# A transformer-like block on one Trainium2 core: first norm on tokens-on-partitions tiles turned by TensorE, and stores issued by the producing engine

## Chip, cores and metric

The kernel runs on 1 core of one Trainium2 chip. The metric is the device time of one execution in microseconds (us), the median of the runs shown.

## What is computed

One layer on x (1024 tokens x 1024 channels, f32), cut to what bears on the change:

```
mod = silu(c) @ w_ada + b_ada            # shift1, scale1, gate1, shift2, scale2, gate2
h   = rms_norm(x, norm1_g) * (1 + scale1) + shift1
z   = h @ w_in                           # q latent | kv latent | rope key | conv GLU input | gate logits
u   = glu_a * sigmoid(glu_b); u = causal_depthwise_conv(u) ...; y_b = silu(layer_norm(u)) @ w_pw_out
y_a = attention(...) @ w_o_mla
x   = x + gate1 * ((sigmoid(g_a) * y_a + sigmoid(g_b) * y_b) @ w_out)
x   = x + gate2 * (relu(h2 @ w_ff1) ** 2 @ w_ff2)     # h2: second norm and modulation
```

## The kernel before

Every f32 product is made of three products of rounded parts: an operand is split into `hi` (ScalarE, `copy`, L108) and `lo` = operand - `hi` (`split`, L114), and `mm` (L117) is called for hi*hi, lo*hi and hi*lo. So one result bank of 128x512 takes 3 matmuls for each 128 of depth.

**The first stage** (L289 to L390, 0 to 85 us). x is read transposed (`x_t`, channels on partitions) as eight tiles `x0..x7` of 128x1024, in two halves `c` of 512 tokens. `norm(c)` squares the eight tiles (ScalarE, L319, L322), adds the squares (VectorE, L323), sums over partitions with 8 small matmuls against ones, takes a reciprocal root on VectorE and ScalarE (`rsqrt`, L218) and spreads it to all partitions with four turns on TensorE (`spread`, L227). For each depth block k of 128 channels, `modulation(k)` reads two rows of blocks of `w_ada` (`ada_load`, 512 KB each, six buffers) and forms `sc` and `sh` on VectorE (`ada`, L282); `scaled` multiplies x by `sc` and the spread norm (L347); `h_tile(k, c)` adds `sh`, makes `hhi` (ScalarE, L353) and `hlo` (VectorE, L354) and issues the 12 matmuls for the first four output tiles, z0. For 8 k and 2 c that makes 192 matmuls into 8 banks of 512: `z` (four) and two pairs `k`.

**The next stages** (85 to 450 us): further tiles of `w_in` (`z_tile`), of which four more feed the GLU (`glu`) and the convolution (`conv`, VectorE, GpSimd, ScalarE), and the gate tiles. `gate` (L404) applies the sigmoid on ScalarE and stores it with `nc.sync.dma_start` (L409). Weight tiles are prefetched by `weights`/`fetch` (L126 to L140) with two buffers each for raw, hi and lo.

**The first MLP product** (820 to 1050 us). By a Strassen-like scheme, a step m of 16 reads two raw weight tiles (`prepare_w`, L976, `raw`, L889), forms their sums and splits on VectorE and ScalarE, and multiplies five products (seven from m = 12), each of 12 matmuls into one of six `z` banks; VectorE adds the results up (`sum_of`, L1013). `right_operands` (L1034) forms four differences on GpSimd. `keep` (L1010) stores each finished block with `nc.sync.dma_start`; `p1_d` (L1029) stores a partial product.

Each engine runs its instructions in one fixed order, written down at build time by a list scheduler. SyncE's queue does too: a DMA there waits for its data and for a free buffer, and what stands behind it waits too.

Of the kernel before, what the change touches and what calls it, by code (L numbers as in the profile page):

```python
# [17 lines left out]
S = 1024  # L18
D = 1024
# [56 lines left out]
def block_kernel(ctx: ExitStack, tc: tile.TileContext, a: dict, out: bass.AP):  # L76
# [46 lines left out]
    def plan(src, width=D, hi_eng=None, lo_eng=None):  # L123
        loads.append((src, width, hi_eng or nc.scalar, lo_eng or nc.gpsimd))
# [16 lines left out]


    for t in range(2 * KC - 4):
        plan(a["w_in"][t], lo_eng=nc.vector if t < 2 else None)
    first = [sum(FILL[:n]) for n in range(len(FILL) + 1)]

    def plan_gates(n):
# [92 lines left out]
    def halves(ts):  # L240
        return [[t[:, cs(0)], t[:, cs(1)]] for t in ts]
# [33 lines left out]
    def ada_load(j):  # L275
        w = ada_pool.tile([P, D], F32, name="wada", bufs=6)
        nc.sync.dma_start(w, a["w_ada"][blk(j)])
        return w
# [5 lines left out]
        )  # L284

    phase = ExitStack()
    phase.enter_context(psum(z=4, k=2))


    z0 = [[None, None] for _ in range(4)]  # L290
    z0_pairs = []
    with tc.tile_pool(name="xp", bufs=1, **right) as xp:
        xs = [xp.tile([P, S], F32, name=f"x{k}") for k in range(KD)]
        rs = xp.tile([P, S], F32, name="rs")
        w0 = []
        w0r = []
        aw = []

        def load_x(c):
            for k in range(KD):  # L300
                nc.sync.dma_start(xs[k][:, cs(c)], a["x_t"][blk(k)][:, cs(c)])

        def load_w(k):
            aw.append((ada_load(KD + k), ada_load(k)))
            raw = xp.tile([P, C], F32, name="w0raw", bufs=2)
            nc.sync.dma_start(raw, a["w_in0"][k])
            w0r.append(raw)
# [6 lines left out]
        def norm(c):  # L314
            acc = xp.tile([P, C], F32, name="xacc", bufs=2)
            for k in range(KD):
                x_k = xs[k][:, cs(c)]
                if k == 0:
                    nc.scalar.activation(acc, x_k, AF.Square)  # L319
                else:  # L320
                    sq = xp.tile([P, C], F32, name="sq", bufs=3)
                    nc.scalar.activation(sq, x_k, AF.Square)  # L322
                    nc.vector.tensor_tensor(acc, acc, sq, ALU.add)  # L323
            shi = xp.tile([P, C], F32R, name="shi")
            slo = xp.tile([P, C], F32R, name="slo")
            split(shi, slo, acc, nc.scalar, nc.vector)
            st, rb = halves([pair("k")])[0]
            r1 = rsqrt(xp, stat_cols(shi, slo, NB // 2, st=st), D, [P, NB // 2], f"r1{c}")
            spread(r1, [rb])
            copy(nc.scalar, rs[:, cs(c)], rb)  # L330
            return rb

        mod1 = []

        def modulation(k, rb=None):
# [3 lines left out]
            nc.vector.tensor_scalar(sc, sc, 1.0, v("g1", k), ALU.add, ALU.mult)  # L339
            mod1.append((sc, sh))  # L340
            if rb is not None:
                scaled(k, 0, rb)
            ada(sh, k, aw[k][1])

        def scaled(k, c, rb):
            x_k = xs[k][:, cs(c)]
            nc.vector.scalar_tensor_tensor(x_k, x_k, mod1[k][0], rb, ALU.mult, ALU.mult)  # L347

        def h_tile(k, c):
            sh = mod1[k][1]  # L350
            x_k = xs[k][:, cs(c)]
            hi, lo = h_hi[k][:, cs(c)], h_lo[k][:, cs(c)]
            nc.scalar.activation(hi, x_k, AF.Identity, bias=sh)  # L353
            nc.vector.scalar_tensor_tensor(lo, x_k, sh, hi.bitcast(F32), ALU.add, ALU.subtract)  # L354
            whi, wlo = w0[k]
            for m in range(4):
                if k == 0 and c == 0:
                    z0[m][c] = bank("z")
                elif k == 0:
                    if m % 2 == 0:  # L360
                        z0_pairs.append(pair("k"))
                    z0[m][c] = z0_pairs[m // 2][:, cs(m % 2)]
                o = z0[m][c]
                mm(o, whi[:, blk(m)], hi, k == 0, False)
                mm(o, whi[:, blk(m)], lo, False, False)
                mm(o, wlo[:, blk(m)], hi, False, k == KD - 1)

        load_x(0)
# [3 lines left out]
        load_x(1)  # L372
        for k in range(KD):
            load_w(k)
        rb = norm(0)
        first_norm = last_rsqrt[0]
        norm(1)
        second_norm = last_rsqrt[0]
        split_w(0)
        with tc.issue_after(first_norm.ins):  # L380
            modulation(0, rb)
        for k in range(KD):
            h_tile(k, 0)
            if k + 1 < KD:
                split_w(k + 1)
                with tc.issue_after(second_norm.ins):
                    modulation(k + 1)
                scaled(k + 1, 0, rs[:, cs(0)])
            scaled(k, 1, rs[:, cs(1)])
            h_tile(k, 1)  # L390
        sel_f = xp.tile([P, C], F32, name="sel_f", tag="sq", bufs=3)[:, 0:13 * NH + P]
# [12 lines left out]
    def gate(d, new):  # L404
        o = z_tile()
        for c in range(2):
            s_t = new("sg")
            nc.scalar.activation(s_t, o[c], AF.Sigmoid)  # L408
            nc.sync.dma_start(s_d[d][:, cs(c)], s_t)  # L409

    def gates(n, new):
        for d in range(first[n], first[n + 1]):
# [5 lines left out]
    with tc.tile_pool(name="cv", bufs=1, **right) as cv:  # L418
# [17 lines left out]
        def conv(i, u):

# [31 lines left out]
        conv(2, us[2])
# [835 lines left out]
```

## Time and profile before

| | |
|---|---|
| median of 3 runs | 1402.04 us (1401.58 to 1405.19) |
| the profiled execution | 1403.63 us, its span 1401.5 us |
| TensorE busy | 1335.7 us (95%) |
| VectorE, ScalarE, GpSimd busy | 995.6, 680.4, 402.2 us |
| mean granted TensorE clock | 0.988 |
| DMA | 234.72 MB, 167 GB/s over the span |

The span runs from the first to the last instruction; the profiled execution's own time is 2.1 us longer, and 1.6 us over the median. An engine that is busy 95% of the span bounds the kernel almost everywhere, so what counts is where it is idle or runs at a lower clock, and which other engine ends that.

### The profile page before, as it was taken

The page shows a single profiled execution, that of the slowest core. Times are in us where ns is not written, and L with a number is a line of the kernel's source. Part 1 is how long each engine was busy: PE and PEld are TensorE (multiplying, and loading weights), DVE is VectorE, ACT ScalarE, POOL GpSimd, SP SyncE. Part 2 cuts the span into 40 slices and gives each one's busy share as a digit, 9 for nine tenths or more (in the row PEclk, how much of TensorE's full clock was granted, in tenths as well). Part 3 has the DMA queues.
Part 4 walks back from the last instruction along what each step waited for, and adds up shares of the span by engine and source line. Part 5 has one row for each costly group of instructions (what it writes and reads, how often), then busy time and mean ns, then how long its engine had stood idle before and what let it go on. Part 6 is the DMA issues. An engine that isn't in the chain of part 4 may idle for free. (4 is left out here: it accounts for less than half of the span.)

```text
span 1401.5 us, 17857 instructions
## 1 busy us (share of the span) xinstructions
PE 1335.7 (95%) x6160; PEld 1088.4 (78%) x6160; DVE 995.6 (71%) x1488; ACT 680.4 (49%) x1107; POOL 402.2 (29%) x280
## 2 busy tenths in 40 slices
PE   3899999999998999999999999989999999999998
PEld 2687888887676888878788878767778887887787
DVE  7969997955346788767546788766675459848854
ACT  6345422246556777753345763343455444444342
POOL 0049932244554655425100003334333100000000
PEclk9999999999999999999999999999999999999999
DMA  9611227731475323127546555566656678633442
GB/s 358 218 45 53 84 93 277 260 121 60 137 253 188 121 91 121 47 77 259 190 135 205 188 186 208 197 195 210 211 176 234 236 227 279 215 98 90 140 139 76
DMA packets 106186, 234.72 MB, mean 167 GB/s; under 512 B 12016, under 2 KB 12272, under 8 KB 106096
## 3 DMA queue, kind: packets, MB, share of 16 engines
q1 hardware_dynamic: 106096, 233.58, 49.3%
q8 instruction: 48, 0.79, 0.2%
q14 instruction: 42, 0.34, 0.1%
HBM read 169.57 MB, written 63.96 MB: 167 GB/s over the span
## 5 line engine op out<-in xcount | busy, mean ns | idle before, releaser
L117 PE MATMUL z<-hhi,whi 128*128 128x512 f32 x384 | 152.7, 399 | 0.4 <-ACT sg L408 0.4
L117 PE MATMUL z<-hlo,whi 128*128 128x512 f32 x384 | 152.4, 397 | 0.0
L117 PE MATMUL z<-hhi,wlo 128*128 128x512 f32 x384 | 152.1, 397 | 0.0
L1040 POOL TENSOR_TENSOR t<-u 128x512 f32<-128x512 f32 x16 | 23.0, 1440 | 316.4 <-DMA wraw<-in_w_ff 171.4
L108 ACT ACTIVATE whi<-wraw 128x1024 fp32r<-128x1024 f32 x71 | 74.9, 1055 | 59.7 <-PE z L117 46.4
L453 DVE SCALAR_TENSOR_TENSOR k<-u,vec,k 128x1024 f32<-128x1024 f32 x84 | 100.9, 1281 | 0.0
L114 POOL TENSOR_TENSOR wlo<-wraw,whi 128x1024 fp32r<-128x1024 f32 x25 | 62.6, 2503 | 115.0 <-ACT whi L108 110.3
L117 PEld LDWEIGHTS z<-hhi,whi 128*128 128x128 f32 x384 | 72.3, 188 | 19.6 <-ACT sg L408 1.0
L117 PEld LDWEIGHTS z<-hhi,wlo 128*128 128x128 f32 x384 | 72.3, 188 | 18.2
L117 PEld LDWEIGHTS z<-hlo,whi 128*128 128x128 f32 x384 | 72.4, 188 | 17.4
L114 DVE TENSOR_TENSOR wlo<-wraw,whi 128x1024 fp32r<-128x1024 f32 x46 | 60.7, 1319 | 26.2 <-ACT whi L108 26.2
L282 DVE CUSTOM_DVE_ANT_0 wada<-wada,c_act,vec 128x1024 f32<-128x1024 f32 x48 | 66.0, 1410 | 7.8 <-DMA wada<-in_w_ada 7.8
L1006 ACT ACTIVATE u<-u 128x512 f32<-128x512 f32 x64 | 39.9, 628 | 63.1 <-DVE u L1015 61.2
L446 POOL TENSOR_TENSOR accp<-accp,prc 128x1024 f32<-128x1024 f32 x28 | 67.4, 2413 | 9.8 <-ACT prc L445 8.6
L117 PE MATMUL z<-ghT,hi 128*128 128x512 f32 x160 | 62.9, 393 | 1.7 <-DVE u L1015 1.7
L117 PE MATMUL z<-glT,hi 128*128 128x512 f32 x160 | 62.5, 391 | 0.0
L117 PE MATMUL z<-ghT,lo 128*128 128x512 f32 x160 | 62.3, 390 | 0.0
L117 PE MATMUL z<-l_whi,h_whi 128*128 128x512 f32 x148 | 57.9, 391 | 4.1 <-DVE l_whi L114 4.1
L1015 DVE TENSOR_TENSOR u<-z,u 128x512 f32<-128x512 f32 x80 | 52.9, 684 | 10.4 <-PE z L117 7.2
L117 PE MATMUL z<-l_wraw,h_wraw 128*128 128x512 f32 x152 | 59.6, 392 | 0.0
L117 PE MATMUL z<-h_wraw,l_wraw 128*128 128x512 f32 x152 | 59.2, 390 | 0.0
L117 PE MATMUL z<-l_wlo,h_wlo 128*128 128x512 f32 x148 | 57.7, 390 | 0.1
(363 smaller groups left out, 3893.8 us busy)
## 6 DMA issues: line engine op xcount, KB each, us to landing
wada<-in_w_ada SPq DMA_DIRECT2D x48, 512.0 KB, 5.9
wraw<-in_w_ff SPq DMA_DIRECT2D x44, 512.0 KB, 4.2
fraw<-fdT SPq DMA_DIRECT2D x64, 256.0 KB, 2.7
wraw<-in_w_in SPq DMA_DIRECT2D x24, 512.0 KB, 3.6
fd<-u SPq DMA_DIRECT2D x48, 256.0 KB, 2.6
fdT<-t SPq DMA_DIRECT2D x48, 256.0 KB, 4.3
fraw<-fd SPq DMA_DIRECT2D x48, 256.0 KB, 2.8
w<-in_w_ff SPq DMA_DIRECT2D x48, 256.0 KB, 3.8
```

The source lines that it names most:

```text
L108: eng.activation(o, i, AF.Copy)
L114: lo_eng.tensor_tensor(lo, src, hi.bitcast(F32), ALU.subtract)
L117: nc.tensor.matmul(o, l, r, start=start, stop=stop)
L282: nc.vector.tensor_tensor_reduce(out=w, in0=w, in1=c_act, scale=1.0, scalar=v("b_ada", j), op0=ALU.mult, op1=ALU.add, accum_out=dst,)
L446: nc.gpsimd.tensor_tensor(accp, accp, pr, ALU.add)
L453: nc.vector.scalar_tensor_tensor(t, u[:, j:j + S], w(j), t, ALU.mult, ALU.add)
L1006: nc.scalar.activation(f, f, AF.Relu)
L1015: last_sum[0] = nc.vector.tensor_tensor(t, x, y, ALU.add)
L1040: nc.gpsimd.tensor_tensor(t3, f22, f12, ALU.subtract)
```

## The change

x is loaded as it lies in memory (`x_n`, tokens on partitions, eight tiles `xn0..xn7` of 128x1024). ScalarE squares a tile and sums it along its row in one instruction (`accum_out`), in groups of two, two and four tiles; the reciprocal root then is one number per partition, and VectorE, ScalarE or GpSimd scales each tile in place. For each k and c TensorE turns four 128x128 blocks into a bank `x` (`turned`); ScalarE applies `sc` and `sh` there and copies `hi` out; VectorE makes `lo`. `multiply0` issues the matmuls, 12 for c = 0 and 6 for c = 1 while k runs; the other 48 follow behind. The loads of `w_ada` for k = 0 stand ahead of x. `lo` of all four GLU weight tiles is made by VectorE. The GLU's tiles 2 and 3 are multiplied half by half (`two_tiles`) and stand ahead of the first convolution. The stores of `gate`, of `p1_d` and of three of seven kinds of `keep` are issued by ScalarE, the other four kinds by GpSimd. Removed lines stand in the listing above.

```diff
-        plan(a["w_in"][t], lo_eng=nc.vector if t < 2 else None)
+        plan(a["w_in"][t], lo_eng=nc.vector)
...
-    phase.enter_context(psum(z=4, k=2))
+    phase.enter_context(psum(z=4, k=1, x=2))
...
+        def load_x(bs):
+            for b in bs:
+                nc.sync.dma_start(xn[b], a["x_n"][blk(b)])
...
+        def norm(bs, engines):
+            for b in bs:
+                junk = xp.tile([P, D], F32, name="junk", bufs=2)
+                nc.scalar.activation(junk, xn[b], AF.Square, accum_out=ssq1[:, b:b + 1])
+            done = None
+            r = rsqrt(xp, ssq1[:, bs[0]:bs[-1] + 1], D, [P, len(bs)], f"r1{bs[0]}")
+            for n, (b, eng) in enumerate(zip(bs, engines)):
+                if eng is nc.scalar:
+                    eng.activation(xn[b], xn[b], AF.Copy, scale=r[:, n:n + 1])
                 else:
+                    o = eng.tensor_scalar(xn[b], xn[b], r[:, n:n + 1], 1.0, ALU.mult, ALU.mult)
+                    done = o if eng is nc.vector else done
+            return done
...
+        def turned(k, c):
+            o = bank("x")
+            for b in range(C // P):
+                nc.tensor.transpose(o[:, blk(b)], xn[c * (C // P) + b][:, blk(k)], ident)
+            sc, sh = mod1[k]
             hi, lo = h_hi[k][:, cs(c)], h_lo[k][:, cs(c)]
+            nc.scalar.activation(o, o, AF.Identity, scale=sc, bias=sh)
+            copy(nc.scalar, hi, o)
+            made.append(nc.vector.tensor_tensor(lo, o, hi.bitcast(F32), ALU.subtract))
+
+        def multiply0(k, c, ms):
             whi, wlo = w0[k]
+            hi, lo = h_hi[k][:, cs(c)], h_lo[k][:, cs(c)]
+            for n, (w, x) in enumerate(((whi, hi), (wlo, hi), (whi, lo))):
+                for m in ms:
+                    mm(z0[m][c], w[:, blk(m)], x, k == 0 and n == 0, k == KD - 1 and n == 2)
...
+        load_ada(0)
+        load_x(range(4))
+        load_w(0)
+        load_ada(1)
+        load_x(range(4, NB))
+        load_w(1)
+        for k in range(2, KD):
+            load_ada(k)
+            last_load = load_w(k)
...
+        order = [(0, 0), (1, 0), (0, 1), (1, 1)] + [(k, c) for k in range(2, KD) for c in range(2)]
+        turned(0, 0)
+        for n, (k, c) in enumerate(order):
+            if n == 0:
+                second_norm = norm((4, 5, 6, 7), (nc.vector, nc.scalar, nc.gpsimd, nc.vector))
+            if n + 1 < len(order):
+                nk, nch = order[n + 1]
+                if nch == 0:
...
+                        modulation(nk)
+                    split_w(nk)
+                turned(nk, nch)
+            multiply0(k, c, range(4) if c == 0 else range(2))
+        for m in range(2, 4):
+            z0[m][1] = bank("x")
+            for k in range(KD):
+                multiply0(k, 1, (m,))
...
-            nc.sync.dma_start(s_d[d][:, cs(c)], s_t)
+            nc.scalar.dma_start(s_d[d][:, cs(c)], s_t)
...
+        def two_tiles():
+            ws = [weights(), weights()]
+            return lambda c: [gemm(w, halves(h_hi), halves(h_lo), KD, chunks=(c,))[0] for w in ws]
...
-    def keep(n, m, t):
-        nc.sync.dma_start(f_d[n][m], t)
+    def keep(n, m, t, eng=nc.scalar):
+        eng.dma_start(f_d[n][m], t)
...
-            nc.sync.dma_start(p1_d[m], p1[m])
+            nc.scalar.dma_start(p1_d[m], p1[m])
...
-        keep("T3", m, t3)
+        keep("T3", m, t3, nc.gpsimd)
```

T1, T2 and T4 are changed as T3 is. The orders below number lines by each kernel's own file.

**TensorE, first stage.** Before, from the last matmuls of k = 0 on (`hhi`, `hlo`: parts of h; `w0hi`, `w0lo`: of the weights; `r11`: the second norm, being spread):

```order
L117 MATMUL z_324<-hhi0_84,w0lo0_305 128x512
L117 MATMUL z_328<-hlo0_92,w0hi0_304 128x512
L117 MATMUL z_328<-hhi0_84,w0lo0_305 128x512
L236 MATMUL k_281<-ident_65,r11_291 128x128 x4
L117 MATMUL z_316<-hhi1_85,w0hi1_332 128x512
L117 MATMUL z_320<-hhi1_85,w0hi1_332 128x512
L117 MATMUL z_324<-hhi1_85,w0hi1_332 128x512
L117 MATMUL z_328<-hhi1_85,w0hi1_332 128x512
L117 MATMUL k_345<-hhi0_84,w0hi0_304 128x512
L117 MATMUL k_352<-hhi0_84,w0hi0_304 128x512
```

Now, at k = 2 and k = 3, c = 0 and 1 (`x_384`, `x_398`: banks with turned blocks):

```order
L117 MATMUL z_235<-hlo2_94,w0hi2_337 128x512
L117 MATMUL z_236<-hlo2_94,w0hi2_337 128x512
L117 MATMUL z_237<-hlo2_94,w0hi2_337 128x512
L117 MATMUL z_238<-hlo2_94,w0hi2_337 128x512
L345 MATMUL x_384<-ident_65,xn0_120 128x128
L345 MATMUL x_384<-ident_65,xn1_121 128x128
L345 MATMUL x_384<-ident_65,xn2_122 128x128
L345 MATMUL x_384<-ident_65,xn3_123 128x128
L117 MATMUL k_239<-hhi2_86,w0hi2_337 128x512 x2
L117 MATMUL k_239<-hhi2_86,w0lo2_338 128x512 x2
L117 MATMUL k_239<-hlo2_94,w0hi2_337 128x512 x2
L345 MATMUL x_398<-ident_65,xn4_124 128x128
```

Turns of four token blocks now stand between the groups of matmuls, one group ahead of their use.

**ScalarE, first stage.** Before, around the first `hhi` (`rs`: the spread norm):

```order
L108 ACTIVATE rs_128<-k_231 128x512
L353 ACTIVATE hhi0_84<-x0_120,sh0_308 128x512
L212 ACTIVATE r11_291<-r11_ms_290 128x4
L108 ACTIVATE w0hi1_332<-w0raw_166 128x512
L108 ACTIVATE whi_698<-wraw_696 128x1024
L108 ACTIVATE whi_704<-wraw_702 128x1024
L108 ACTIVATE rs_128<-k_281 128x512
L108 ACTIVATE w0hi2_373<-w0raw_172 128x512
L108 ACTIVATE w0hi3_412<-w0raw_178 128x512
L353 ACTIVATE hhi1_85<-x1_121,sh1_336 128x512
```

Now, up to the first two `hhi` (`junk`: a square that is not read; `ssq1`: its row sum):

```order
L212 ACTIVATE r12_221<-r12_ms_220 128x2
L328 ACTIVATE xn3_123<-xn3_123,r12_221 128x1024
L323 ACTIVATE junk_248,ssq1_128<-xn4_124 128x1024
L348 ACTIVATE x_240<-x_240,sh0_196,sc0_197 128x512
L323 ACTIVATE junk_250,ssq1_128<-xn5_125 128x1024
L108 ACTIVATE hhi0_84<-x_240 128x512
L348 ACTIVATE x_278<-x_278,sh1_269,sc1_270 128x512
L323 ACTIVATE junk_252,ssq1_128<-xn6_126 128x1024
L108 ACTIVATE hhi1_85<-x_278 128x512
L323 ACTIVATE junk_254,ssq1_128<-xn7_127 128x1024
L108 ACTIVATE w0hi1_274<-w0raw_147 128x512
```

The squares of the second half of the tokens now stand between the steps that make `hhi` of the first half.

**GpSimd, first MLP product**, step m = 0 before (`t3`, `t2`, `t4`: differences; `fdT3_0`: T3 of step 0 in memory):

```order
L1040 TENSOR_TENSOR t3_8003<-u_7986,u_7992 128x512
L1042 TENSOR_TENSOR u_7992<-u_7992,f11_8000 128x512
L1045 TENSOR_TENSOR t2_8008<-u_7986,u_7992 128x512
L1049 TENSOR_TENSOR t4_8012<-u_7996,t2_8008 128x512
L1040 TENSOR_TENSOR t3_8124<-u_8107,u_8113 128x512
```

And now:

```order
L1051 TENSOR_TENSOR t3_8031<-u_8014,u_8020 128x512
L1022 DMA fdT3_0_6143<-t3_8031 128x512
L1053 TENSOR_TENSOR u_8020<-u_8020,f11_8028 128x512
L1022 DMA fdT1_0_6111<-u_8020 128x512
L1056 TENSOR_TENSOR t2_8036<-u_8014,u_8020 128x512
L1022 DMA fdT2_0_6127<-t2_8036 128x512
L1060 TENSOR_TENSOR t4_8040<-u_8024,t2_8036 128x512
L1022 DMA fdT4_0_6159<-t4_8040 128x512
L1051 TENSOR_TENSOR t3_8152<-u_8135,u_8141 128x512
```

Each difference is followed by its store, on GpSimd's own queue.

## Rows read from the trace of the kernel before

**Rows 1.** The page: span and busy time by engine.

```profile
span 1401.5 us, 17857 instructions
...
PE 1335.7 (95%) x6160; PEld 1088.4 (78%) x6160; DVE 995.6 (71%) x1488; ACT 680.4 (49%) x1107; POOL 402.2 (29%) x280
```

**Rows 2.** Stretches: engines' busy us (instructions), PEclk, DMA share, GB/s.

```profile
0.00:24.00 24.00, 6.74 (x28) 6.03 (x28) 15.91 (x33) 16.59 (x30) 1.11 (x9) 1.00 0.93 337
24.00:85.00 61.00, 50.62 (x198) 39.89 (x199) 47.11 (x87) 20.50 (x30) 2.25 (x2) 0.92 0.60 216
...
30.00:40.00 10.00, 2.93 (x6) 1.82 (x6) 10.00 (x18) 4.75 (x7) 0.00 (x0) 0.66 1.02 392
...
450.00:500.00 50.00, 47.70 (x318) 43.44 (x318) 39.43 (x93) 35.32 (x76) 26.55 (x28) 1.00 0.34 108
...
60.00:310.00 250.00, 250.00 (x1093) 201.49 (x1092) 212.49 (x232) 95.81 (x116) 127.47 (x54) 1.00 0.36 130
820.00:1050.00 230.00, 219.91 (x936) 174.39 (x935) 165.42 (x202) 98.52 (x144) 77.46 (x52) 1.00 0.57 196
```

**Rows 3.** Timeline, TensorE, 24 to 85: start, us, instruction, idle before it.

```profile
24.05 2.07 PE L117 MATMUL z<-hhi,w0hi 128*128 128x512 f32 x4 [1.69 <-ACT hhi L353]
...
34.91 2.08 PE L117 MATMUL z<-hhi,w0hi 128*128 128x512 f32 x4 [5.67 <-ACT hhi L353]
...
41.08 0.51 PE L117 MATMUL z<-hlo,w0hi 128*128 128x512 f32 x1 [3.25 <-DVE hlo L354]
...
43.52 0.63 PE L117 MATMUL z<-hlo,w0hi 128*128 128x512 f32 x1
43.94 0.63 PE L117 MATMUL z<-hhi,w0lo 128*128 128x512 f32 x1
...
84.53 0.40 PE L117 MATMUL k<-hhi,w0lo 128*128 128x512 f32 x1
84.76 0.39 PE L117 MATMUL z<-hhi,whi 128*128 128x512 f32 x1
```

**Rows 4.** DMA in 0 to 110 us, 40 slices of 2.75 us.

```profile
GB/s 84 272 289 392 389 405 407 405 410 408 396 410 405 378 328 279 201 261 267 277 346 322 15 0 0 171 19 162 34 0 0 0 0 0 0 0 92 98 0 6
```

**Rows 5.** ScalarE by line and shape: busy us, mean ns, idle before.

```profile
L108 ACT ACTIVATE whi<-wraw 128x1024 fp32r<-128x1024 f32 x71 | 74.9, 1055 | 59.7 <-PE z L117 46.4 <-DMA wraw<-in_w_ff 9.1 <-PE t L117 1.8
...
L108 ACT ACTIVATE ph<-t 128x512 fp32r<-128x512 f32 x48 | 27.9, 594 | 11.9 <-PE t L786 6.8 <-PE v L117 4.0 <-DVE nb L757 0.9
...
L937 ACT ACTIVATE x<-x,mod,amp 128x512 f32<-128x512 f32 x16 | 12.2, 808 | 0.8 <-DVE x L936 0.8
...
L763 ACT ACTIVATION_READ_ACCUMULATOR prs<-s,nb,rqs 128x1 f32 x32 | 6.3, 198 | 0.0
```

**Rows 6.** Timeline, VectorE, first norm and modulation.

```profile
18.68 0.16 DVE L216 SCALAR_TENSOR_TENSOR r<-r_t,r 128x4 f32<-128x4 f32 x1
...
25.83 1.28 DVE L282 CUSTOM_DVE_ANT_0 wada<-wada,c_act,vec 128x1024 f32<-128x1024 f32 x1
```

**Rows 7.** Timeline, TensorE in the attention: nine turns in a row.

```profile
475.95 1.16 PE L786 MATMUL t<-ident,pr 128*128 128x128 f32 x9
```

**Rows 8.** Waits in 820 to 1050 us: total, times, longest.

```profile
PE z L117 <- DVE u L1015: 8.3, 9, 1.9
...
DVE wy L973 <- DMA wraw<-in_w_ff: 44.8, 14, 4.8
...
SPq L891 <- DVE lo L114: 41.8, 13, 5.8
```

**Rows 9.** Timelines of GpSimd and of SyncE's queue in that stretch.

```profile
930.76 1.29 POOL L1040 TENSOR_TENSOR t<-u 128x512 f32<-128x512 f32 x1 [10.90 <-ACT u L1007]
...
934.88 1.29 POOL L1049 TENSOR_TENSOR t<-u,t 128x512 f32<-128x512 f32 x1
944.73 1.31 POOL L1040 TENSOR_TENSOR t<-u 128x512 f32<-128x512 f32 x1 [8.56 <-ACT u L1007]
...
917.14 0.32 SPq L1011 DMA_DIRECT2D fdT<-u  x1
```

More of the change, by code (lines that the diff above doesn't have):

```diff
@@ L286, in block_kernel @@
     phase = ExitStack()
-    phase.enter_context(psum(z=4, k=2))
+    phase.enter_context(psum(z=4, k=1, x=2))
     z0 = [[None, None] for _ in range(4)]
-    z0_pairs = []
     with tc.tile_pool(name="xp", bufs=1, **right) as xp:
-        xs = [xp.tile([P, S], F32, name=f"x{k}") for k in range(KD)]
-        rs = xp.tile([P, S], F32, name="rs")
+        xn = [xp.tile([P, D], F32, name=f"xn{b}") for b in range(NB)]
+        ssq1 = xp.tile([P, NB], F32, name="ssq1")
         w0 = []
@@ L297, in block_kernel, with load_ada @@
         aw = []
-        def load_x(c):
-            for k in range(KD):
-                nc.sync.dma_start(xs[k][:, cs(c)], a["x_t"][blk(k)][:, cs(c)])
+        mod1 = []
+        made = []
+        def load_ada(k):
+            aw.append((ada_load(KD + k), ada_load(k)))
+        def load_x(bs):
+            for b in bs:
+                nc.sync.dma_start(xn[b], a["x_n"][blk(b)])
         def load_w(k):
[L304 to L307, printed above, removed]
+            w_raw = xp.tile([P, C], F32, name="w0raw", bufs=2)
+            w0r.append(w_raw)
+            return nc.sync.dma_start(w_raw, a["w_in0"][k])
         def split_w(k):
@@ L312, in split_w, with modulation @@
             w0.append((hi, lo))
[L314 to L319, printed above, removed]
-                else:
[L321 to L335, printed above, removed]
+        def norm(bs, engines):
[7 more added lines that the diff above has]
+                    eng.activation(xn[b], xn[b], AF.Copy, scale=r[:, n:n + 1])
+                else:
+                    o = eng.tensor_scalar(xn[b], xn[b], r[:, n:n + 1], 1.0, ALU.mult, ALU.mult)
+                    done = o if eng is nc.vector else done
+            return done
+        def modulation(k):
             sh = xp.tile([P, 1], F32, name=f"sh{k}")
@@ L339, in modulation @@
             nc.vector.tensor_scalar(sc, sc, 1.0, v("g1", k), ALU.add, ALU.mult)
+            ada(sh, k, aw[k][1])
             mod1.append((sc, sh))
[L341 to L351, printed above, removed]
+        def turned(k, c):
[3 more added lines that the diff above has]
+            sc, sh = mod1[k]
             hi, lo = h_hi[k][:, cs(c)], h_lo[k][:, cs(c)]
-            nc.scalar.activation(hi, x_k, AF.Identity, bias=sh)
-            nc.vector.scalar_tensor_tensor(lo, x_k, sh, hi.bitcast(F32), ALU.add, ALU.subtract)
+            nc.scalar.activation(o, o, AF.Identity, scale=sc, bias=sh)
+            copy(nc.scalar, hi, o)
+            made.append(nc.vector.tensor_tensor(lo, o, hi.bitcast(F32), ALU.subtract))
+        def multiply0(k, c, ms):
             whi, wlo = w0[k]
[L356 to L368, printed above, removed]
+            hi, lo = h_hi[k][:, cs(c)], h_lo[k][:, cs(c)]
[11 more added lines that the diff above has]
+            last_load = load_w(k)
         cb = spread(c_col, halves([pair("k")])[0])
@@ L371, in block_kernel @@
             copy(nc.scalar, c_act[:, cs(c)], cb[c])
[L372 to L378, printed above, removed]
-        split_w(0)
[L380 to L391, printed above, removed]
+        modulation(0)
+        norm((0, 1), (nc.vector, nc.scalar))
+        first_norm = norm((2, 3), (nc.vector, nc.scalar))
+        split_w(0)
+        for m in range(4):
+            z0[m][0] = bank("z")
+        z0[0][1], z0[1][1] = halves([pair("k")])[0]
+        order = [(0, 0), (1, 0), (0, 1), (1, 1)] + [(k, c) for k in range(2, KD) for c in range(2)]
[6 more added lines that the diff above has]
+                if nch == 0:
+                    with tc.issue_after((first_norm if nk == 1 else second_norm if nk == 2 else made[2 * nk - 3]).ins):
+                        modulation(nk)
[6 more added lines that the diff above has]
+                multiply0(k, 1, (m,))
+        sel_f = xp.tile([P, C], F32, name="sel_f", tag="w0raw", bufs=2)[:, 0:13 * NH + P]
         nc.sync.dma_start(sel_f, a["sel"])
@@ L425, in taps, with glu @@
             return lambda j: v("conv_w", i * TAPS + j)
-        def glu(i, oa, ob):
+        def glu(part):
             u = cv.tile([P, S + 32], F32, name="u", bufs=4)
@@ L430, in glu @@
             for c in range(2):
+                oa, ob = part(c)
                 sb = cv.tile([P, C], F32, name="sb", bufs=2)
-                nc.scalar.activation(sb, ob[c], AF.Sigmoid)
-                nc.vector.tensor_tensor(u[:, PAD + c * C:PAD + (c + 1) * C], oa[c], sb, ALU.mult)
-            return u
+                nc.scalar.activation(sb, ob, AF.Sigmoid)
+                nc.vector.tensor_tensor(u[:, PAD + c * C:PAD + (c + 1) * C], oa, sb, ALU.mult)
+            return u
+        def two_tiles():
+            ws = [weights(), weights()]
+            return lambda c: [gemm(w, halves(h_hi), halves(h_lo), KD, chunks=(c,))[0] for w in ws]
         def conv(i, u):
@@ L458, in cv_half @@
             return cv.tile([P, C], F32, name=name, tag="ev", bufs=4)
-        us = [glu(0, z0[0], z0[1]), glu(1, z0[2], z0[3])]
-        pend = [z_tile(), z_tile()]
+        us = [glu(lambda c, i=i: (z0[2 * i][c], z0[2 * i + 1][c])) for i in range(2)]
+        phase.close()
+        phase.enter_context(psum(z=4, k=2))
+        with tc.issue_after(last_load.ins):
+            us.append(glu(two_tiles()))
+        us.append(glu(two_tiles()))
         conv(0, us[0])
-        us.append(glu(2, *pend))
-        pend = [z_tile(), z_tile()]
         conv(1, us[1])
-        us.append(glu(3, *pend))
         for d in range(GA):
@@ L1040, in right_operands @@
         nc.gpsimd.tensor_tensor(t3, f22, f12, ALU.subtract)
-        keep("T3", m, t3)
+        keep("T3", m, t3, nc.gpsimd)
         nc.gpsimd.tensor_tensor(f12, f12, f11, ALU.subtract)
-        keep("T1", m, f12)
+        keep("T1", m, f12, nc.gpsimd)
         t2 = p1_tile("t2")
         nc.gpsimd.tensor_tensor(t2, f22, f12, ALU.subtract)
-        keep("T2", m, t2)
+        keep("T2", m, t2, nc.gpsimd)
         keep("21", m, f21)
@@ L1049, in right_operands @@
         nc.gpsimd.tensor_tensor(t4, f21, t2, ALU.subtract)
-        keep("T4", m, t4)
+        keep("T4", m, t4, nc.gpsimd)
     NP = FF // P // 2
@@ L1211, in _layout @@
     f = np.float32
+    a["x_n"] = np.ascontiguousarray(i["x"][0])
     a["x_t"] = np.ascontiguousarray(i["x"][0].T)
```

## The prediction

> **What bounds the kernel now.** I read four views. The page first: TensorE is busy 1335.7 of 1401.5 us [rows 1], so nothing is won but where it idles or runs slowly. Then the stretches: from 60 to 310 us it is busy all 250.00 us at clock 1.00, while in the first 85 us it is busy only 6.74 of 24 and 50.62 of 61, and the clock of the second part is 0.92 (0.66 from 30 to 40 us) [rows 2]. That is some 28 us of idle time in one place. Third, TensorE's timeline there [rows 3]: the first matmul of z0 starts at 24.05; it idles 5.67 us before 34.91 (for `hhi` from ScalarE) and 3.25 us before 41.08 (for `hlo` from VectorE); at 43.52 the matmuls are 0.42 us apart, the lower of TensorE's two levels (1.2 GHz), and at the end 0.23 us apart, the upper one (2.4 GHz). z0 ends at 84.76. Since nothing waits on TensorE for 250 us after the start, what z0's end gains goes on unchanged to 310 us. Fourth, the waits of the first MLP product: TensorE idles 10.1 of 230 us there [rows 2], 8.3 of it for VectorE's sums, and VectorE waits 44.8 us for raw weights [rows 8].
>
> The sum is made against the profiled execution, 1403.63 us, which is 1.59 us over the median of 1402.04. About 0.3% of this time, 4.2 us, is what a measurement can tell from no change.
>
> **When the first matmul can start now.** Loads run in SyncE's order: constants (0.11 MB), two blocks of `w_ada`, then x's first four tiles, each 0.52 MB. Adding up the slices of [rows 4] (0.23 MB by 2.75 us, 0.98 by 5.5, 1.77 by 8.25, 2.85 by 11, then 0.39 to 0.40 MB per us), the four tiles are there at 7.9, 9.4, 10.7 and 12.0 us, and the next four by 20.5. On ScalarE a square of 1024 columns takes 1.06 us and reading a row sum 0.20 [rows 5]. The scaling of the second tile stands between the squares, so the fourth square, due at 12.0, ends near 14.1. Then follow, in the new order: a weight split (0.5), the root (0.2), four small VectorE steps at 0.16 to 0.2 [rows 6] (0.8), the scaling of the fourth tile (1.06), the turns, hidden under the square of a tile of the second half that is placed there (1.06), `sc` and `sh` in place (0.81), another such square with its sum read (1.25) and the copy to `hhi` (0.59) [rows 5]. 14.1 + 6.3 = **20.4 us**, against 24.05. Bounds: 17.2 if no foreign square stood between, 24 if the tiles come later than this sum has them.
>
> **From there to the end of z0.** The 192 matmuls stay: 192 x 0.23 = 44.2 us. Removed are 16 sums over partitions and 8 turns of the norm, all before or inside waits, so worth nothing by themselves. Added are 64 turns of 128x128; eight come before the first matmul. The trace has the same instruction in the attention: nine in 1.16 us, 0.129 each in a row [rows 7], so 56 x 0.129 = 7.2 us. One wait is left that I can see: when k = 0 and 1 of the first half are through, the turned blocks of the second half must pass ScalarE twice 0.81 and 0.59 before the next matmul; some 2.0 us. After that the turns run a group ahead, and what the other engines need per k is below TensorE's 18 x 0.23 + 8 x 0.129 = 5.2 us: VectorE two `w_ada` reductions (2 x 1.28 [rows 6]), one weight split and two `hlo` of half that width (0.64 each), 4.5 us; ScalarE 2 x (0.81 + 0.59) + 0.5 = 3.3 us. That cover is thin on VectorE: one more 1.3 us step per k and it would be the bound. Loads per k are 1.3 MB, 3.3 us at 0.4 MB per us. Last the clock: 0.92 over 61 us is 4.9 us lost, after two starts from idle (24.05 and 34.91); now there is one start, so 2.4 us. The sum: 20.4 + 44.2 + 7.2 + 2.0 + 2.4 = **76.2 us**, against 84.76: a gain of 8.6. The same sum for before, 24.05 + 44.2 + 5.67 + 3.25 + 4.9, gives 82.1; 2.7 us of smaller waits and turns stay unexplained, so the way of adding is good to about 3 us.
>
> A single turn's duration in the profile is longer than 0.129, because turns overlap. The Trainium skill ("TensorE: Matmul & The Clock Gate", Part 4) gives about 275 ns for one in a kernel. By that figure the 56 turns would be an estimated 15.4 us, and all but 0.4 of the gain would be gone; [rows 7] show nine in 1.16 us, and the sum goes by them.
>
> **After z0.** Tiles 2 and 3 of the GLU are the same 192 matmuls in another order. The third weight tile's buffer comes free 5.6 us before its first use (24 matmuls at 0.23), where two whole tiles lay between before; a ScalarE copy (1.06), a VectorE split and up to four convolution steps of 1.3 ahead of it fit in, barely: 0, at most 1.5 us lost. The two splits moved from GpSimd to VectorE are hidden by TensorE's 250 busy us, in which VectorE is busy 212. Convolution starts 8 us earlier with z0. I take 0.
>
> **The stores.** For the gates, 32 stores of 0.32 us of issue [rows 9] move from SyncE to ScalarE: 10 us beside 95.8 busy of 250; TensorE waits for nothing there. Nothing. In the first MLP product, SyncE's queue loses its waits for finished blocks, and the weight loads behind them could go earlier. But the loads themselves wait 41.8 us for VectorE to free a buffer [rows 8], and that stays. Gain between 0 and the 8.3 us of [rows 8]; loss: three ScalarE issues of 0.32 per step, and four on GpSimd, whose price no row shows. From below it is SyncE's 0.32, from above a GpSimd instruction of this size, 1.29. GpSimd's four differences run from 930.76 to 936.17 and the next come at 944.73 [rows 9]: 8.56 us free per step, 2.14 per store. Either price fits. I take 0 for the stores, with -6 and +4 as ends.
>
> The Trainium skill ("DMA: Bandwidth & Descriptors", Issuing engines are not separate DMA queues) says that issuing from several engines saves only the sequencer's time, usually small beside the transfer. By it the stores are worth 0, which the 41.8 us for buffers bear out.
>
> **Forecast.** 1403.63 - 8.6 = 1395.0 in a run like the profiled one; 1.59 less for the median: **1393.4 us**, its own range 1387 to 1399.
>
> **Rivals.**
> - *The stores do pay.* Weight loads land earlier because blocks to be stored no longer queue with them, and VectorE's waits (14 of them, 44.8 us) shrink by 0.6 us each, which ends most of TensorE's 8.3 us. 5 us more: 1388. For it: loads and stores alternate in one queue. Against: the buffers. Chance 0.16.
> - *New waits take the place of the old.* VectorE's 4.5 of 5.2 us per k leaves little, `hlo` stands behind the reductions in VectorE's fixed order, and TensorE may again wait the 8.9 us of [rows 3] and start from idle twice: 76.2 + 6.9 + 2.4 = 85.5, no gain, 1402.7. Against: 14 adds and 16 scalings, by the listing, leave VectorE in this stage. Chance 0.13.
> - *GpSimd becomes the bound* (slower). If a store costs GpSimd more than 2.14 us, its queue falls behind the matmuls in the twelve steps of five products, the blocks it reads are held, the reload of `f11` waits for a buffer and the weights behind it in SyncE's queue too. At 2.6 us that is 12 x 4 x 0.46 = 22 us: 1415. Against: a difference of this size, which reads and writes every element, takes GpSimd 1.29 us [rows 9]. Chance 0.07. The Trainium skill (same page, SWDGE vs HWDGE vs iDMA) says that GpSimd's cores compute such descriptors in software; no run here shows their price yet.
> - *The clock stays at the lower level* (slower). If turns between the matmuls kept it at 1.2 GHz until the last turn, some 144 matmuls at 0.42 instead of 0.23 add 27 us: 1420. Against: from 450 to 500 us turns stand among the matmuls and the clock is 1.00 [rows 2, 7]. Chance 0.04. The Trainium skill's Part 4, named above, has this rule: transposes do not count as work for the clock; by the 1.00 just named the trace does not bear it out in a mix.
>
> **The numbers.** The forecast has 0.60. 8 in 10 lie between 1385 (a start at 17.2 and paying stores) and 1402 (most of the new waits). Faster by over 4.2 us: the forecast without its slow edge and the paying stores, 0.73; the same: new waits and that edge, 0.16; slower: 0.11.
>
> **What would show it.** First z0 matmul at 19 to 21.5 us; z0 over, and matmuls with `whi` begun, at 74 to 79; clock over 0.95 from 24 to 85; one wait of about 2 us near 29; turns about 0.13 apart; no wait on TensorE from 80 to 300. In the first MLP product VectorE's 44.8 us for weights within 5 of that, and GpSimd's stores in a second queue. I am wrong if z0 ends after 82, or if TensorE's waits in the first MLP product change by over 6 us.

## The result and the profile after

The changed kernel takes 1411.21 us (median of 6 runs, 1407.31 to 1413.12) against 1401.99 for the kernel before; the ratio is 1.0054 [1.0037, 1.0072], slower by some 8 us. The forecast was 1393.4. The profiled execution took 1409.85 us.

The page of the changed kernel, span and busy time, against [rows 1]:

```profile
span 1408.1 us, 17884 instructions
...
PE 1342.9 (95%) x6200; PEld 1092.9 (78%) x6200; DVE 991.1 (70%) x1467; ACT 690.0 (49%) x1123; POOL 427.4 (30%) x343
```

Its stretches, with the columns of [rows 2] (busy us and instructions of TensorE, its weight loads, VectorE, ScalarE, GpSimd; granted clock, DMA share, GB/s):

```profile
24.00:85.00 61.00, 56.44 (x261) 45.17 (x261) 40.47 (x72) 32.24 (x47) 4.84 (x4) 0.97 0.59 205
60.00:310.00 250.00, 248.50 (x1100) 200.85 (x1099) 210.93 (x227) 97.04 (x118) 124.39 (x52) 1.00 0.38 134
820.00:1050.00 230.00, 212.58 (x878) 167.90 (x877) 164.31 (x193) 94.18 (x135) 98.84 (x104) 0.97 0.54 188
930.00:935.00 5.00, 2.93 (x14) 2.09 (x13) 4.06 (x6) 1.67 (x2) 1.95 (x3) 1.00 0.60 236
935.00:940.00 5.00, 5.00 (x16) 3.96 (x15) 4.17 (x6) 2.96 (x6) 0.00 (x1) 0.66 0.48 157
```

The first stage is better than before, as forecast. The first MLP product is where the time goes: 878 matmuls in 230 us where there were 936. The 58 that are missing are 13 us at 0.23 each. TensorE idles 17.4 us there (10.1 before), and the granted clock is 0.97 (1.00 before).

TensorE's timeline of the changed kernel in the first stage, against [rows 3]:

```profile
19.95 2.08 PE L117 MATMUL z<-hhi,w0hi 128*128 128x512 f32 x4 [2.54 <-ACT hhi L108]
...
30.27 1.06 PE L117 MATMUL k<-hhi,w0hi 128*128 128x512 f32 x2 [1.92 <-ACT hhi L108]
...
41.78 1.20 PE L117 MATMUL z<-hhi,w0hi 128*128 128x512 f32 x4 [0.95 <-ACT hhi L108]
...
48.21 1.20 PE L117 MATMUL z<-hhi,w0hi 128*128 128x512 f32 x4 [1.14 <-ACT hhi L108]
...
59.46 1.20 PE L117 MATMUL z<-hhi,w0hi 128*128 128x512 f32 x4 [0.56 <-ACT hhi L108]
...
79.90 0.39 PE L117 MATMUL z<-hhi,whi 128*128 128x512 f32 x1
```

z0 starts at 19.95 and is over at 79.90, where the first matmul with `whi` begins: 4.9 us earlier than before. (In the ten other profiled executions with this start, those of the experiments below, it is over between 80.84 and 81.72.) Further on, TensorE is idle 1.5 us between 60 and 310 (none before) and 18.0 us between 310 and 820 (19.5 before). So some 5 us are still in hand at 820, and the first MLP product loses them and 7 more.

The waits of the changed kernel from 820 to 1050 us (total, times, longest), against [rows 8]:

```profile
DVE wy L984 <- DMA wraw<-in_w_ff: 47.0, 12, 5.5
PE z L117 <- DVE u L1026: 13.3, 8, 2.1
PE z L117 <- ACT p L108: 2.7, 1, 2.7
```

These totals hardly tell it: VectorE's wait for weights grew by 2 us. One step does. Timelines of SyncE's queue, GpSimd and VectorE in the changed kernel (start, us, instruction, idle before it):

```profile
941.86 0.33 SPq L902 DMA_DIRECT2D wraw<-in_w_ff  x1
...
940.00 1.29 POOL L1051 TENSOR_TENSOR t<-u 128x512 f32<-128x512 f32 x1 [7.73 <-ACT u L1018]
941.58 0.56 POOL L1022 DMA_DIRECT2D fdT<-t  x1 [0.30 <-POOL t L1051]
942.16 1.31 POOL L1053 TENSOR_TENSOR u<-u,f 128x512 f32<-128x512 f32 x1
...
946.53 1.30 POOL L1060 TENSOR_TENSOR t<-u,t 128x512 f32<-128x512 f32 x1
...
956.43 1.29 POOL L1051 TENSOR_TENSOR t<-u 128x512 f32<-128x512 f32 x1 [7.74 <-ACT u L1018]
...
940.46 1.37 DVE L114 TENSOR_TENSOR s4l<-wraw,s4h 128x512 fp32r<-128x512 f32 x1 [1.29 <-ACT s4h L108]
...
947.15 1.24 DVE L984 TENSOR_TENSOR wy<-wraw 128x512 f32<-128x512 f32 x1 [4.72 <-DMA wraw<-in_w_ff]
948.43 0.69 DVE L985 TENSOR_TENSOR wy<-wy,wraw 128x512 f32<-128x512 f32 x1
...
956.89 1.38 DVE L114 TENSOR_TENSOR s4l<-wraw,s4h 128x512 fp32r<-128x512 f32 x1 [1.29 <-ACT s4h L108]
```

This is a closed loop. `s4l` ends (941.83) and frees a raw buffer; SyncE issues the next load into it at once (941.86); `wy` starts when it has landed (947.15, 5.29 us later); VectorE works through the step until `s4l` ends again (958.27, 11.1 us later). The next step has the same length: GpSimd's rows stand 16.43 us apart (940.00, 956.43), and so do the two `s4l` (940.46, 956.89). VectorE's waits in it are for the load (4.72 us) and for ScalarE's `s4h` (1.29), none for TensorE. Three things in these rows suggest what made the loop longer: with a store between them GpSimd's differences start 2.2 us apart, not 1.4 [rows 9] (a store waits 0.30 us for its own difference and takes 0.56 of issue, which moves the next difference by 0.8), so the fourth starts 6.5 us after the first, not 4.1; it then runs beside `wy`, which takes 1.24 us where its like take 0.69; and the load takes 5.3 us.

The kernel before has the same loop, and a shorter one: 4.45 us from the load to `wy` and 10.41 from there to the end of `s4l` (961.48).

```profile
946.62 0.33 SPq L891 DMA_DIRECT2D wraw<-in_w_ff  x1
...
951.07 0.69 DVE L973 TENSOR_TENSOR wy<-wraw 128x512 f32<-128x512 f32 x1 [3.89 <-DMA wraw<-in_w_ff]
...
960.12 1.36 DVE L114 TENSOR_TENSOR s4l<-wraw,s4h 128x512 fp32r<-128x512 f32 x1 [1.29 <-ACT s4h L108]
```

The longer step also costs clock. TensorE's timeline of the changed kernel behind one such wait:

```profile
933.95 0.50 PE L117 MATMUL z<-ghT,whi 128*128 128x512 f32 x1 [2.07 <-DVE u L1026]
934.29 0.40 PE L117 MATMUL z<-glT,whi 128*128 128x512 f32 x1
...
935.38 0.63 PE L117 MATMUL z<-ghT,wlo 128*128 128x512 f32 x1
935.81 0.63 PE L117 MATMUL z<-ghT,whi 128*128 128x512 f32 x1
```

After 2.07 us of idleness the matmuls still come 0.23 apart for 1 us and then 0.43 apart (TensorE's lower level, 1.2 GHz) for 3.4: the row 935 to 940 above has clock 0.66. The stretch has four such dips, an estimated 6.8 us together (5 us at 0.66 lose 1.7); the kernel before has none there. Not every wait brings one: of the six longest waits in the stretch (1.98 to 2.65 us), the two before 966.80 and 983.23 (2.06 us each) were followed by none.

### The profile page after: what moved, and what is told of

The parts are those of the page before. It is cut to its first block, busy times and chain, and to the rows that moved or that the text cites. A ratio compares the mean times of both kernels' runs of the same rounds, so it can differ in the third digit from the quotient of the medians.

```text
span 1408.1 us, 17884 instructions
## 1 busy us (share of the span) xinstructions
PE 1342.9 (95%) x6200; PEld 1092.9 (78%) x6200; DVE 991.1 (70%) x1467; ACT 690.0 (49%) x1123; POOL 427.4 (30%) x343
## 5 line engine op out<-in xcount | busy, mean ns | idle before, releaser
L114 POOL TENSOR_TENSOR wlo<-wraw,whi 128x1024 fp32r<-128x1024 f32 x23 | 57.6, 2504 | 115.2 <-ACT whi L108 115.2
L282 DVE CUSTOM_DVE_ANT_0 wada<-wada,c_act,vec 128x1024 f32<-128x1024 f32 x48 | 69.7, 1490 | 7.4 <-DMA wada<-in_w_ada 4.1
L1026 DVE TENSOR_TENSOR u<-z,u 128x512 f32<-128x512 f32 x80 | 52.9, 685 | 14.5 <-PE z L117 12.3
```

The costliest lines, as they stand in the source:

```text
L282: nc.vector.tensor_tensor_reduce(out=w, in0=w, in1=c_act, scale=1.0, scalar=v("b_ada", j), op0=ALU.mult, op1=ALU.add, accum_out=dst,)
L1026: last_sum[0] = nc.vector.tensor_tensor(t, x, y, ALU.add)
```

## The experiments

The theory: GpSimd's stores, standing between its differences, push the last difference onto VectorE's `wy` and lengthen the loop. Rivals: the moved start shifts later stages into a bad phase; ScalarE's stores delay the loads; issuing from GpSimd costs wherever it stands; the order that the list scheduler wrote. Runs of one batch share the runs of the kernel before; ratios are to those.

### The parts alone

**Start alone.** From the changed kernel, all stores back:

```diff
-            nc.scalar.dma_start(s_d[d][:, cs(c)], s_t)
+            nc.sync.dma_start(s_d[d][:, cs(c)], s_t)
-    def keep(n, m, t, eng=nc.scalar):
+    def keep(n, m, t, eng=nc.sync):
-            nc.scalar.dma_start(p1_d[m], p1[m])
+            nc.sync.dma_start(p1_d[m], p1[m])
-        keep("T3", m, t3, nc.gpsimd)
+        keep("T3", m, t3)
```

(T1, T2 and T4 as T3.)

> The start of the change with every store issued by SyncE again. Theory A (the stores turn the first MLP product into a slower loop; the start is sound): z0 ends near 79.9 as after the whole change, TensorE is idle about 10 of the 230 us from 820 to 1050 at clock 1.00 as before, and the time is 1402.0 - 4.9 (z0) - 1.4 (310 to 820 us) = about 1396. Theory B (the new start only shifts the later stages into a bad phase, the stores are innocent): near 1411.

1396.75 us, ratio 0.9946 [0.9927, 0.9965]: theory A. The start is worth some 7 us (6.8 by the medians, 7.6 by the ratio): z0 is over 3.9 us earlier (80.84), and in the first MLP product TensorE idles 6.7 us, less than the 10 expected.

**Without GpSimd's stores.** The changed kernel, with T1 to T4 stored by SyncE (`keep("T3", m, t3, nc.sync)` and so on):

> The whole change, but the four kinds of blocks that GpSimd makes are stored by SyncE again; ScalarE keeps its stores. In the written order VectorE's s4l (which frees the buffer of the next weight load) now stands ahead of the sums in all of the steps m = 1 to 11, where it stands behind four sums in five steps of the whole change and four of the kernel before. Theory A1 (that place of s4l sets the loop load - VectorE - load, and GpSimd's stores moved it): TensorE's idle in 820 to 1050 falls below the 10.1 us of before, clock 1.00, time 1388 to 1393. Theory A2 (ScalarE's stores on a queue of their own delay the loads): idle stays near 17, time above 1405.

1398.73 us, 0.9962 [0.9943, 0.9981], which neither theory had. ScalarE's stores alone are not the loss, but A1 was wrong about the order. `s4l` early cuts VectorE's waits for weights from 47.0 to 18.8 us, and VectorE's busy time rises from 164.3 to 197.6 us, because its work for the weights now stands beside GpSimd's differences; the steps stay at 15 to 16 us. Stretch, and timelines of GpSimd and VectorE, of that run:

```profile
820.00:1050.00 230.00, 222.06 (x944) 175.83 (x943) 197.64 (x204) 103.93 (x147) 89.22 (x54) 1.00 0.56 193
...
931.98 1.80 POOL L1051 TENSOR_TENSOR t<-u 128x512 f32<-128x512 f32 x1 [6.00 <-ACT u L1018]
933.86 1.63 POOL L1053 TENSOR_TENSOR u<-u,f 128x512 f32<-128x512 f32 x1
935.57 1.62 POOL L1056 TENSOR_TENSOR t<-u 128x512 f32<-128x512 f32 x1
...
932.54 1.79 DVE L996 TENSOR_TENSOR wraw<-wraw 128x512 f32<-128x512 f32 x1
934.25 1.79 DVE L997 TENSOR_TENSOR wraw<-wraw,wy 128x512 f32<-128x512 f32 x1
935.96 0.68 DVE L1026 TENSOR_TENSOR u<-z,u 128x512 f32<-128x512 f32 x1
```

L996 takes 1.79 us beside a difference, and 0.68 us alone (950.99 in the next run). The sum `u` at 935.96, which has one input in TensorE's bank `z`, runs beside a difference too and takes 0.68.

**GpSimd's stores, without ScalarE's.** The start alone, with T1 to T4 on GpSimd:

> The start of the change and GpSimd's four stores, with ScalarE's stores issued by SyncE again. s4l stands behind four sums in seven steps. Theory A1: the loss is here: about 17 us idle in 820 to 1050, 1408 to 1412. Theory A2 (ScalarE's stores make the loss): about 1396.

1409.07 us, 1.0027 [1.0013, 1.0042]: the loss is here. Timelines of GpSimd and VectorE in that run:

```profile
949.13 1.38 POOL L1060 TENSOR_TENSOR t<-u,t 128x512 f32<-128x512 f32 x1
...
948.67 0.69 DVE L984 TENSOR_TENSOR wy<-wraw 128x512 f32<-128x512 f32 x1 [3.63 <-DMA wraw<-in_w_ff]
949.40 1.67 DVE L985 TENSOR_TENSOR wy<-wy,wraw 128x512 f32<-128x512 f32 x1
950.99 0.68 DVE L996 TENSOR_TENSOR wraw<-wraw 128x512 f32<-128x512 f32 x1
```

The step of 0.69 us that falls beside GpSimd's last difference takes 1.67 and ends 0.56 us after it (951.07, 950.51), as `wy` does in the changed kernel (948.39, 947.83).

**Stores alone.** The kernel before with only its stores moved:

> The kernel before with only the stores moved (start unchanged). If the two parts simply add up: 1402.0 + 14 (idle +7.3 us and about 6.8 us of lower clock in the first MLP product) = about 1416. If the stores hurt only together with the new start: 1402.

1415.32 us, 1.0075 [1.0052, 1.0097]: the stores cost 10.5 to 12 us with the old start too. With the start's 0.9946 this makes 1.0021, where the whole change has 1.0054 [1.0037, 1.0072]. That is at the edge of what the intervals separate, so whether the parts simply add up is open.

### One place changed

**Stores behind.** The start and GpSimd's stores, as above, but:

```diff
-        keep("T3", m, t3, nc.gpsimd)
...
-        keep("T1", m, f12, nc.gpsimd)
...
-        keep("T2", m, t2, nc.gpsimd)
...
-        nc.gpsimd.tensor_tensor(t4, f21, t2, ALU.subtract)
-        keep("T4", m, t4, nc.gpsimd)
+        last = nc.gpsimd.tensor_tensor(t4, f21, t2, ALU.subtract)
+        with tc.issue_after(last.ins):
+            keep("T3", m, t3, nc.gpsimd)
+            keep("T1", m, f12, nc.gpsimd)
+            keep("T2", m, t2, nc.gpsimd)
+            keep("T4", m, t4, nc.gpsimd)
```

> As the run of GpSimd's stores alone (1409.1), but in each step the four differences stand together and their four stores behind them. Theory L (the stores stretch GpSimd's row of differences: each costs it 0.30 waiting for its own difference and 0.56 of issue, so the last difference runs beside VectorE's wy, which takes up to 2.2 us instead of 0.69 inside the loop load - VectorE - load): the row is 5.4 us again, wy 0.69 to 0.7 in the settled steps, chain from wy to the end of s4l 10.4 to 10.8 instead of 11.5 to 12.2, time 1397 to 1400. Theory Q (what costs is that GpSimd issues them, or the second queue, wherever they stand): 1406 to 1410.

1396.15 us, 0.9947 [0.9932, 0.9962]: theory L, and 1 us better than it expected; 11 to 13 us (by the ratios and by the medians) come from the place of four stores. VectorE's order in the settled steps is that of the run with the stores in between (1409.07), so the order is not the cause.

**The whole change with the stores behind**, ScalarE's stores kept:

> The whole change, with the four stores on GpSimd behind the four differences of a step. With ScalarE's stores issued by SyncE this order gave 1396.2. If ScalarE's stores cost nothing of their own: 1395 to 1398, and from the issue of the second weight load to wy 4.0 to 4.4 us. If they delay the loads, as the 5.0 to 5.5 us of the whole change against 4.15 to 4.35 of GpSimd's stores alone suggest: 0.9 us in each of some 6 settled steps, 1400 to 1403.

1392.75 us, 0.9922 [0.9905, 0.994], better than either expectation. Timelines of GpSimd and VectorE in that run, and the stretch:

```profile
938.08 1.29 POOL L1057 TENSOR_TENSOR t<-u,t 128x512 f32<-128x512 f32 x1
939.31 0.56 POOL L1022 DMA_DIRECT2D fdT<-t  x1
939.87 0.54 POOL L1022 DMA_DIRECT2D fdT<-u  x1
940.40 1.07 POOL L1022 DMA_DIRECT2D fdT<-t  x2
...
939.23 0.69 DVE L984 TENSOR_TENSOR wy<-wraw 128x512 f32<-128x512 f32 x1 [3.16 <-DMA wraw<-in_w_ff]
939.96 0.69 DVE L985 TENSOR_TENSOR wy<-wy,wraw 128x512 f32<-128x512 f32 x1
...
820.00:1050.00 230.00, 227.23 (x976) 182.12 (x975) 168.87 (x211) 105.55 (x153) 112.96 (x112) 1.00 0.58 201
```

GpSimd issues its stores while `wy` runs, and `wy` takes 0.69: the issue does not hold VectorE up, only a difference does. TensorE idles 2.8 us of 230.

The loop in the settled steps of these kernels, in us (load: from the issue of the last load to `wy`; VectorE: from `wy` to the end of `s4l`; step: from one start of GpSimd's differences to the next; time: the median):

| kernel | load | VectorE | step | time |
|---|---|---|---|---|
| before | 4.2 to 4.45 | 10.4 to 10.8 | 14.8 to 14.9 | 1402 |
| whole change | 5.0 to 5.5 | 11.0 to 11.35 | 16.4 | 1411.2 |
| start alone | 4.0 to 4.2 | 10.4 to 10.8 | 14.5 to 14.8 | 1396.75 |
| whole change, GpSimd's stores on SyncE | 4.7 to 5.6 | 9.9 to 10.4 | 14.6 to 16.5 | 1398.7 |
| GpSimd's stores, no ScalarE's | 4.15 to 4.35 | 11.5 to 12.15 | 15.7 to 16.5 | 1409.1 |
| the same, stores behind | 4.0 to 4.2 | 10.55 to 10.7 | 14.6 to 14.8 | 1396.15 |
| whole change, stores behind | 3.7 to 3.9 | 10.55 to 10.7 | 14.3 to 14.5 | 1392.75 |

With GpSimd's stores and not ScalarE's, the loop grows on VectorE alone, by some 1 to 1.5 us. In the whole change VectorE gives only 0.6 of the 1.6 us that a step is longer; the other 1.0 is the load. The slower loads (5.0 to 5.5 us, 5.2 to 5.8 with the stores alone) have a GpSimd store (941.58) and a ScalarE store (941.64) issued just ahead of the load on other queues. With GpSimd's stores bunched, ScalarE's make nothing slower. But a GpSimd store is not needed: with GpSimd's stores on SyncE, between the loads, and ScalarE's where they were, the loads take 4.7 to 5.6 us too (4.2 to 4.45 before, with all stores on SyncE). Whether the bandwidth shared with such stores is the reason was not tried by itself.

**Gates alone.** The start, and only the gates' 32 stores on ScalarE:

> The start of the change, and of the stores only the 32 of the gates issued by ScalarE (those of the first MLP product by SyncE). TensorE waits for nothing in the gates' stage, so no difference from the start alone: 1396 to 1398. If ScalarE's issues there delay the convolution or the weights: 1399 or more.

1396.96 us, 0.9947 [0.9927, 0.9968]: nothing, as forecast.

### The loop cut

`s4` gets a tile of its own, so that a raw weight tile comes free early; NP1, the buffers of the p1 blocks, falls from 8 to 6 to make room:

```diff
-        nc.vector.tensor_tensor(p[:, cs(1)], p[:, cs(1)], y[:, cs(1)], ALU.subtract)
+        s4 = small_pool.tile([P, C], F32, name="s4", bufs=2)
+        nc.vector.tensor_tensor(s4, p[:, cs(1)], y[:, cs(1)], ALU.subtract)
...
-        split(*w["S4"], p[:, cs(1)], nc.scalar, nc.vector)
+        split(*w["S4"], s4, nc.scalar, nc.vector)
```

In the whole change as it was:

> The whole change, with the part s4 of the weights written into a tile of its own (two buffers, two fewer buffers for the p1 blocks), so that the raw weight tile comes free 2 to 3 us after wy and not at the end of s4l, 11 us after it. If the loop (s4l ends - the next load lands - wy starts) is what stretches the steps to 16.4 us: VectorE's waits for raw weights fall from 47 to under 30 us, the steps to about 14.5 us, time 1397 to 1402. If something else stretches them (GpSimd's or ScalarE's queue itself): steps stay at 16 us or more and the time at 1409 to 1412.

1397.59 us, 0.9958 [0.9942, 0.9975]: 13.6 us won back without touching a store, VectorE's waits for weights 21.2 us, settled steps 14.3 us. The loop is what carried at least half of the loss, but not all: VectorE's first work on the weights still runs beside GpSimd's third and fourth differences, with 2.25 us here for the 0.68 that L996 takes alone:

```profile
942.68 2.25 DVE L996 TENSOR_TENSOR wraw<-wraw 128x512 f32<-128x512 f32 x1
```

With the start alone:

> The start of the change, all stores issued by SyncE, and s4 in a tile of its own. The loop sets the step there too (14.7 us against 13.8 of matmuls), if the theory holds: 0.9 us in each of some 6 steps and the 5.2 us of TensorE's waits for sums mostly go: 1396.8 - 4 = about 1392. If only the stores make the loop too long: 1397.

1391.3 us, 0.9905 [0.9886, 0.9925]. The kernel before was bound by this loop too: from the first `s4h` matmul of one settled step to that of the next TensorE took 14.85 us, and takes 13.90 here. The same edit gives 5.5 us here and 13.6 in the whole change, so some 6 to 7 us of the stores' cost remain there.

With GpSimd's stores behind, ScalarE's on SyncE:

> GpSimd's four stores behind the four differences, ScalarE's stores issued by SyncE, and s4 in a tile of its own. The stores by themselves cost nothing and the loop is short: 1390 to 1392, as with all stores on SyncE (1391.3). If SyncE's shorter queue helps beyond that: 1386 to 1389.

1391.83 us, 0.9907 [0.9886, 0.9929]: as expected, no more than the run before it.

All together:

> The whole change, GpSimd's stores behind its differences, and s4 in a tile of its own. With the stores behind, TensorE still waits about 1.5 us for sums in 820 to 1050 and steps take 14.4 us (1392.8). If the loop still sets the step: 0.6 us in each of 6 settled steps less, 1388 to 1390. If TensorE's own 13.8 us of matmuls and other stages bound it already, as the 1391.3 and 1391.8 with s4 in its own tile suggest: 1390.5 to 1393.

1389.12 us, 0.9899 [0.9882, 0.9915], faster than both kernels. The time is the one expected if the loop still set the step, but the loop no longer sets it:

```profile
820.00:1050.00 230.00, 228.96 (x991) 185.72 (x990) 179.21 (x210) 106.66 (x153) 123.41 (x115) 1.00 0.60 201
...
928.58 0.40 PE L117 MATMUL z<-gh,s4h 128*128 128x512 f32 x1
...
942.48 0.40 PE L117 MATMUL z<-gh,s4h 128*128 128x512 f32 x1
```

TensorE's step, between the first `s4h` matmuls of two steps, is 13.90 us for 60 matmuls, the 13.8 that I had put down for its own work. It is 13.90 in the two runs before this one too, all three do 991 matmuls in the 230 us, and TensorE idles 1.0 us in each. So the stage runs at TensorE's pace in all three, and a gain of this run over the other two would have to lie elsewhere. (GpSimd's rows stand 13.14 us apart here: they gain on TensorE for some steps and are no measure of its step.)

Its interval overlaps those of the two runs before it and of the whole change with the stores behind, so which is best is open.

## Why the prediction was wrong

**The step that failed** is the last of the costs: "Either price fits. I take 0 for the stores, with -6 and +4 as ends." The stores cost 14 to 15 us (start alone 1396.75, whole change 1411.21), and 10.5 to 12 with the old start. GpSimd's price per store, 0.8 us, lies inside the bounds I had (0.32 to 1.29) and far under the 2.14 at which its row would not fit; GpSimd still idles 7.7 us in every step. That it fits was the wrong question. What counted was where its row ends: beside VectorE's first work on the next weights, in a loop that had no room. The place of the four stores decides it: behind the differences they cost nothing (1396.15; 1392.75 with ScalarE's stores kept). Why the loads came 1.0 us later as well in the whole change stays open.

**What I read past.** Of VectorE's 44.8 us for weights and the loads' 41.8 us for VectorE [rows 8] I wrote "that stays". They are two halves of one ring with two buffers, whose length (14.8 us) already set the step from about 940 us on. Here 1.0 us more on the load and 0.6 on VectorE made every step 1.6 us longer. I had looked only for what the stores could give there.

**The rival "GpSimd becomes the bound"** had the sign and nearly the size (1415), by a mechanism that did not occur: no row shows GpSimd falling behind. The one that fits the rows stands in the Trainium skill ("SBUF — State Buffer", Who interferes with whom): a VectorE instruction with two inputs in SBUF and a GpSimd instruction that reads SBUF exclude each other, and the later one waits until the other is through. The trace agrees: 0.69 became 1.24 and 1.67 us, each ending 0.56 us after GpSimd's difference, and the sum with an input in a bank stayed at 0.68.

**The start** was right in kind and too good by 3.7 us (79.90 for 76.2), by some 5 in the other executions (80.84 to 81.72). First matmul 19.95 for 20.4; the wait near 29 was 1.92 for 2.0. Two terms were too small. "Some 2.0 us" of waits were 1.92 + 0.95 + 1.14 + 0.56 = 4.6: the cover that I called thin on VectorE was thin on ScalarE, which ends each of them. And there were two starts at the lower clock, not one: the first eight matmuls took 3.58 us instead of 1.84, and 30.27 to 34 had clock 0.54 (together 3.5 us for 2.4). The column of the granted clock does not show the first of them: it says 1.00 for 19.95 to 24, where the matmuls come 0.43 to 0.47 apart. So the 0.92 from which the forecast took its 4.9 us [rows 2] lacked such a start as well: before, the eight matmuls from 24.05 took 3.57 us, 1.7 of the 2.7 us left unexplained. Four turns between six matmuls cost 0.45 us, 0.11 each, close to the 0.129 I took. With these terms the sum comes to 78.4; 1.5 us of the 79.90 stay unexplained.

**Right:** nothing for the gates' stores; 0 to 1.5 us lost behind z0 (one wait of 1.50 us before 127.53, for a weight split on GpSimd, though the sign "no wait on TensorE from 80 to 300" did not hold); the start as such pays. The time that I forecast, 1393.4, is that of the whole change with four stores in another place (1392.75), though by another sum and so by luck: the start gave less, and the stores then gave some 3 us (14.4 against 14.7 us a step), near the edge of what the intervals separate. Of the tests I named, z0 before 82 held, and VectorE's waits for weights stayed within 5 us (47.0) while everything else there changed, so that test saw nothing. The other one failed as I had said: TensorE's waits in the first MLP product rose by 7.3 us, over the 6 I had set. The clock's loss, which I had not thought of, came on top.

## What to carry to other kernels

Where a load waits for a buffer and the engine that frees the buffer waits for the load, add up the ring before anything else: where its length is the step's length, nothing on it is free, and a buffer that frees early is worth more than any queue. An instruction moved to an engine with time to spare still shifts what that engine does next; ask which other engine's work it now runs beside. Before stores go to GpSimd, put them behind its arithmetic, not into it.

## What the runs showed of the hardware

- A store on GpSimd that follows its own difference cost 0.30 us of waiting and 0.56 of issue, and moved the next difference by 0.8; bunched behind the differences, 0.54 to 0.56 each with no wait.
- GpSimd issuing a store did not slow VectorE (0.69); GpSimd computing a difference did, up to 2.25 us for 0.68. A sum with one input in TensorE's bank took 0.68 beside a difference too.
- Of the six waits of 1.98 to 2.65 us in the first MLP product of the changed kernel, four were followed, at once or 1 us later, by some 3.4 us at the lower clock, and two were not. Where it fell, a wait of 2 us cost nearly 4.
